# Graph attention: 32 blocks of 128 destinations, taken from two halves of the nodes, in place of 33 blocks of 125

## Chip, core and metric

The kernel runs on one NeuronCore of a Trainium2 chip. The metric is the device time of one execution in microseconds; the median of three runs stands for the kernel. The inputs come from a fixed seed, so every run has the same graph.

## What is computed

One layer of graph attention: 4096 nodes with 64 features, 50,000 edges, 4 heads of 64 output features. Cut to what matters:

```python
x_proj[h] = x @ weight[h]                                # 4 heads
score[h, e] = sum(x_proj[h, src] * att_src[h]) + sum(x_proj[h, dst] * att_dst[h])
score = where(score > 0, score, 0.2 * score)
output[h, dst] += exp(score[h, e]) * x_proj[h, src]      # over the edges e
output[h, dst] /= sum(exp(score[h, e]) over edges to dst) + 1e-8
return output as (4096, 256)
```

## The kernel before

**Two sorts.** Every edge becomes one number, `key`, that holds its source group (16 groups of 256 sources), its destination and its source within the group (lines 700 to 702, in two halves, as the edge list lands). VectorE sorts the keys: `Sorter.rows` sorts each of the 128 rows, `runs` merges 8 rows into each of 16 runs. The sorted runs go to DRAM, each source group is gathered from all 16 runs by an indirect DMA (`group`, lines 365 to 381), and a second sort puts each group's edges in order of destination. Beside the second sort ScalarE counts, for each boundary between blocks of destinations, the keys below it (`below`, line 270: one pass per boundary), TensorE sums these counts, and VectorE turns them into the places where each block begins (`Stretches`).

**Tables.** While the first sort runs, `tables` (lines 383 to 424) prepares what the blocks need: `xT`, the transposed node features, and with it the attention terms of the sources in `xa` and of the destinations in `adb` (line 420, one matmul per 128 sources and one per block of destinations).

**Windows.** A block of destinations meets each of the 16 source groups in one window of `W2` = 128 sorted edges. Eight blocks' windows are fetched by one indirect DMA (line 362), so there are `NI` = ceil(33 / 8) = 5 of them. `unpack(i)` splits the keys of eight blocks into destination and source (two VectorE and two GpSimd instructions, lines 441 to 446) and SyncE stores them to `gat_bins` (line 447).

**Blocks.** `Blocks.run` (line 583) walks over `ND` = 33 blocks of `BD` = 125 destinations; the last has 96. For a block, `load` (line 469) brings its 16 windows to all 128 partitions (1 MB, by SyncE's queue, four buffers), `onehot` (lines 493, 495) compares them with the partition's number, `gather` (lines 514 to 524) lets TensorE pick the features and attention terms of the 16 x 128 edges by one-hot matmuls, and ScalarE takes the exponential and copies `xs` out of PSUM. `weights` and `values` (lines 534, 543) multiply; `sums` (lines 561, 568) adds up the edges of a destination: 16 matmuls for the denominator and 2 x 16 whose moving operand is the one-hot `xs[:, t, 0:BD]`. `Finish` copies the sum out (line 624), projects it with the weights (line 636), divides (lines 641, 649) and stores the rows (line 651). In the last block the two halves are kept apart (`parts`), so that the end of the kernel is short.

The order of the work is written out by hand. In `run`, iteration `b` does `values(b)`, `gather(b + 1)`, `onehot(b + 2)`, `load(b + 4)`, the projection of block `b - 1`, and at last `sums(b)`; iterations 1 and 2 end with `unpack(3)` and `unpack(4)`. SyncE issues its DMAs in that order and holds what stands behind one that waits.

At the end VectorE's word `over` says whether a window was longer than 128 edges (`longest`, lines 746 and 747). If it was, the part below line 776 does the whole aggregation again in loops.

Of the kernel before, what the change touches and what calls it, by code (L numbers as in the profile page):

```python
# [26 lines left out]
W2 = 128  # L27
BD = 125
FINE = 2
# [9 lines left out]
def kernel(ctx: ExitStack, tc: tile.TileContext, x: bass.AP, edge_index: bass.AP,  # L39
# [343 lines left out]
    def tables(pr, pps, pp1):  # L383
# [25 lines left out]
        S.copy(out=xa[:, :, 2 * H:XC], in_=xf[:])  # L409
        xT = pr.tile([Din, ND * BD + P - BD], F32)  # L410
        G.memset(xT[:, N:], 0.0)
        for q in range(NB // 4):
            ps = pps.tile([Din, 4, P], F32, tag="pp")
            for i in range(4):
                T.transpose(out=ps[:, i, :], in_=xf[:, 4 * q + i, :], identity=ident[:])
            S.copy(out=xT[:, 4 * q * P:4 * (q + 1) * P], in_=ps[:])
        for k, (n, step, to) in enumerate(((NB, P, xa[:, :, 0:2 * H]), (ND, BD, adb[:, :, P:AB]))):
            ps = pp1.tile([P, n, H], F32, name=f"at_ps{k}")
            for b in range(n):
                T.matmul(out=ps[:, b, :], lhsT=xT[:, b * step:b * step + P], rhs=uv[:, k, :], start=(b == 0), stop=True,  # L420
                         skip_group_check=True)
            S.copy(out=to[:, :, 0:H], in_=ps[:])
            S.mul(out=to[:, :, H:2 * H], in_=ps[:], mul=ALPHA)
# [30 lines left out]
    class Blocks:  # L454
# [93 lines left out]
        def sums(self, b, k):  # L548
# [3 lines left out]
            if k < 0:  # L552
                self.acc = self.psa.tile([P, AW], F32, name="acc")
                self.to = [self.acc[:, i * BD:(i + 1) * BD] for i in range(2)]
                self.n = BD
                if apart:
                    self.n = N - b * BD
                    self.to = [self.psx.tile([P, CH[0][1], PW], F32, name="ps")[:, 0, 0:self.n] for i in range(2)]
                wv = self.wv.pop(b)
# [7 lines left out]
            for t in range(NT):  # L567
                T.matmul(out=self.to[k], lhsT=val[:, t, k * P:(k + 1) * P], rhs=xs[:, t, 0:self.n],  # L568
                         start=apart and t == 0, stop=(t == NT - 1), skip_group_check=True)
# [39 lines left out]
    class Finish:  # L609
# [29 lines left out]
        def invert(self, b):  # L639
            self.inv = self.fp.tile([P, H], F32, name="inv")  # L640
            V.reciprocal(out=self.inv[0:BD], in_=self.den.pop(b)[0:BD, 2 * BD:AW])

        def give(self, b, parts=1):
            res = self.fp.tile([P, H, Dout], F32, name="res")
            m = min(BD, N - b * BD)
            nh = H // parts
            for k, eng in zip(range(parts), (nc.sync, nc.scalar)):
                h = slice(k * nh, (k + 1) * nh)
                V.tensor_tensor(out=res[0:m, h], in0=av(self.pf[0:m], k * nh * Dout, [Dout, nh], [1, Dout]),
                                in1=av(self.inv[0:m], k * nh, [1, nh], [0, Dout]), op=OP.mult)  # L650
# [34 lines left out]
    with tc.tile_pool(name="sort1", bufs=1) as so1, tc.tile_pool(name="pre", bufs=1) as pr, \  # L685
            tc.tile_pool(name="pps", bufs=2, space=PSUM) as pps, \
            tc.tile_pool(name="pp1", bufs=1, space=PSUM) as pp1:
        sli = so1.tile([P, EL], I32)
        uF = so1.tile([P, EL], F32)
        key = so1.tile([P, L], F32)  # L690
        so = Sorter(so1, key)
# [3 lines left out]
        for e, n in ((0, EH), (EH, EL - EH)):  # L695
# [139 lines left out]
```

## Time and profile before

| | us |
|---|---|
| median of 3 runs | 287.45 |
| lowest and highest of them | 287.11, 287.89 |
| profiled execution, span (its time with what lies around the span isn't listed apart) | 286.5 |

| engine | busy us | share of the span | instructions |
|---|---|---|---|
| TensorE, matmuls | 202.4 | 71% | 3524 |
| TensorE, weight loads | 192.9 | 67% | 3524 |
| VectorE | 259.0 | 90% | 529 |
| ScalarE | 190.8 | 67% | 392 |
| GpSimd | 44.0 | 15% | 81 |

The busy time is an average over stages of quite different kinds. Up to about 112 us the program sorts; from about 128 us to 275 us it walks over the blocks; the rest is the end of the last block and its stores. What bounds each stage is read from the stage's own rows.

### The profile page before, as it was taken

Reading aid. Unit: us, or ns where it says so; the run is one execution under the profiler, and the core shown is the slowest. Engines: PE = TensorE matmul, PEld = TensorE weight load, DVE = VectorE, ACT = ScalarE, POOL = GpSimd, SP = SyncE. Lnnn points to the kernel's source line nnn. Section 1 sums busy time; section 2 is a strip of 40 time slices with the busy share of each in tenths; the row PEclk is TensorE's granted clock in tenths of the full one; section 3 lists DMA queues with packets and bytes.
Section 4 is the critical chain, followed back from the end, with each engine's and each line's share of the span. In section 5 each row is a group of like instructions: output and inputs, shape, how many; then the busy total and the mean of one; then the engine's idle time right before and its main releaser. Section 6 shows DMA issues by size and latency. Waiting matters only on the chain.

```text
span 286.5 us, 8520 instructions
## 1 busy us (share of the span) xinstructions
PE 202.4 (71%) x3524; PEld 192.9 (67%) x3524; DVE 259.0 (90%) x529; ACT 190.8 (67%) x392; POOL 44.0 (15%) x81
## 2 busy tenths in 40 slices
PE   0010899980000046699998999999999999999990
PEld 0010589980000024489998999999999999999980
DVE  5999999994499999899997999999999999999970
ACT  2960620014499956688787888888888888888860
POOL 7883000001100000868700000000000000000000
PEclk9999975555555559999999999999999999999996
DMA  3017000001100001296698576768676767775011
GB/s 112 0 32 136 0 2 0 0 1 38 37 0 0 0 0 40 55 382 207 215 326 321 190 291 214 298 202 302 209 288 222 282 220 282 231 264 188 21 38 43
DMA packets 12687, 40.75 MB, mean 142 GB/s; under 512 B 1840, under 2 KB 8272, under 8 KB 8672
## 3 DMA queue, kind: packets, MB, share of 16 engines
q1 hardware_dynamic: 10128, 37.91, 37.4%
q10 hardware_dynamic: 1808, 1.56, 2.4%
q0 software_dynamic: 704, 0.66, 1.1%
q8 instruction: 29, 0.48, 0.7%
q14 instruction: 18, 0.15, 0.2%
HBM read 35.08 MB, written 5.05 MB: 140 GB/s over the span
## 4 chain that ended last, share of the span: by engine, by line


## 5 line engine op out<-in xcount | busy, mean ns | idle before, releaser
L524 ACT CAST xs<-ps 128x1200 bf16<-128x1200 f32 (+1 forms) x99 | 104.1, 1052 | 0.0
L543 DVE TENSOR_TENSOR val<-xs,wv 128x4096 bf16<-128x4096 bf16 (+3 forms) x37 | 75.6, 2051 | 0.4 <-ACT xs L524 0.2
L568 PE MATMUL acc<-xs,val 128*128 128x125 bf16 x1024 | 62.0, 218 | 1.2 <-issue 1.2
L516 PE MATMUL ps<-adb,oh 128*128 128x136 bf16 x528 | 61.3, 223 | 0.0
L514 PE MATMUL ps<-xa,oh 128*128 128x72 bf16 x528 | 58.8, 196 | 1.7 <-ACT bc L481 1.1
L568 PEld LDWEIGHTS <-val 128*128 128x128 bf16 x1056 | 58.5, 98 | 1.6 <-issue 1.3
L516 PEld LDWEIGHTS <-oh 128*128 128x128 bf16 x528 | 49.0, 98 | 1.5 <-issue 1.4
L514 PEld LDWEIGHTS <-oh 128*128 128x128 bf16 x528 | 47.0, 98 | 1.0 <-DVE oh L493 0.9
L281 PE MATMUL cnt_ps<-sgn,sel 128*128 128x17 f32 (+1 forms) x6 | 1.6, 386 | 59.9 <-ACT sgn L273 40.6
L493 DVE TENSOR_SCALAR oh<-bc,pF 128x4096 bf16<-128x4096 bf16 (+2 forms) x37 | 42.4, 1146 | 0.8 <-ACT bc L481 0.8
L281 PEld LDWEIGHTS cnt_ps<-sgn,sel 128*128 128x128 f32 x6 | 1.4, 318 | 60.0 <-issue 60.0
L522 ACT ACTIVATE ex<-ps 128x96 bf16<-128x96 f32 (+1 forms) x99 | 25.0, 252 | 21.2 <-PE ps L520 21.0
L202 DVE TENSOR_TENSOR sA<-sB 128x256 f32<-128x256 f32 (+2 forms) x104 | 37.2, 399 | 1.5
L202 DVE TENSOR_TENSOR sB<-sA 128x256 f32<-128x256 f32 (+2 forms) x98 | 35.1, 399 | 1.3
L520 PE MATMUL ps<-xa,oh 128*128 128x72 bf16 x528 | 33.3, 197 | 0.1
L520 PEld LDWEIGHTS <-oh 128*128 128x128 bf16 x528 | 26.3, 99 | 0.2 <-DVE oh L495 0.2
L420 PEld LDWEIGHTS at_ps<-uv,xT 64*128 64x128 f32 x130 | 26.0, 311 | 0.2 <-issue 0.2
L420 PE MATMUL at_ps<-uv,xT 64*128 64x4 f32 x130 | 26.1, 338 | 0.0
L495 DVE TENSOR_SCALAR oh<-bc,pF 128x2048 bf16<-128x2048 bf16 (+2 forms) x37 | 25.6, 692 | 0.0
L270 ACT ACTIVATE junk<-kr,nb 128x512 f32<-128x512 f32 x33 | 23.8, 722 | 1.1
L636 PE MATMUL pf<-Wbd,aT 128*128 128x128 f32 x128 | 21.9, 294 | 0.5 <-ACT aT L624 0.5
L561 PEld LDWEIGHTS <-xs 128*128 128x128 bf16 x528 | 18.6, 96 | 1.0 <-issue 0.6
(143 smaller groups left out, 237.3 us busy)
## 6 DMA issues: line engine op xcount, KB each, us to landing
bc<-gat_bins SPq DMA_DIRECT2D x31, 1024.0 KB, 5.1
out_dram<-res SPq DMA_DIRECT2D x32, 125.0 KB
eD<-in_edge_index_dram ACTq DMA_DIRECT2D x2, 195.0 KB, 3.5
eS<-in_edge_index_dram SPq DMA_DIRECT2D x2, 195.0 KB
gat_bins<-tb SPq DMA_DIRECT2D x5, 64.0 KB, 4.8
gat_sorted<-sA SPq DMA_DIRECT2D x1, 256.0 KB, 2.0
gat_sorted<-ki SPq DMA_DIRECT2D x1, 256.0 KB
win<-gat_sorted,to POOLq DMA_INDIRECT x5, 7.9
```

Source lines behind the costliest of these rows:

```text
L202: V.tensor_tensor(out=av(d[:], o, [2 * h, n], [1, h]), in0=av(s[:], 0, [2 * h, n], [1, h]), in1=av(s[:], h, [2 * h, n], [1, h]), op=op)
L270: S.activation(out=junk[:], in_=v, func=ACTF.Sign, bias=nbnd[:, b:b + 1], scale=1.0, accum_out=sgn[:, b:b + 1])
L420: T.matmul(out=ps[:, b, :], lhsT=xT[:, b * step:b * step + P], rhs=uv[:, k, :], start=(b == 0), stop=True, skip_group_check=True)
L493: V.tensor_scalar(out=oh[:, e], in0=bc[:, e], scalar1=pF[:, 0:1], scalar2=None, op0=OP.is_equal)
L495: V.tensor_scalar(out=av(oh[:], (2 * NT + t0) * W2, [W2, nt], [1, W2]), in0=av(bc[:], (2 * t0 + 1) * W2, [2 * W2, nt], [1, W2]), scalar1=p ...
L514: T.matmul(out=ps[:, i, P:P + XC], lhsT=hot(2 * t + 1), rhs=xa[:, 2 * t, :], start=(i % 2 == 0), stop=False, skip_group_check=True)
L516: T.matmul(out=ps[:, i, 0:S0], lhsT=hot(2 * t), rhs=adb[:, b, :], start=False, stop=False, skip_group_check=True)
L520: T.matmul(out=ps[:, i, P:P + XC], lhsT=hot(2 * NT + t), rhs=xa[:, 2 * t + 1, :], start=False, stop=True, skip_group_check=True)
L522: S.activation(out=av(ex[:], 2 * t0, [2, n], [2 * NT, 2 * H], [1, 2]), in_=av(ps[:], P, [PW, n], [1, 2 * H], [0, 2]), func=ACTF.Exp)
L524: S.copy(out=xs[:, t0:t0 + n, 0:P + XC], in_=ps[:, 0:n, 0:P + XC])
L543: V.tensor_tensor(out=av(val[:], h * Dout + t * C, [Dout, nh], [C, n], [1, Din]), in0=av(xs[:], S0 + t * XW, [0, nh], [XW, n], [1, Din]), ...
L568: T.matmul(out=self.to[k], lhsT=val[:, t, k * P:(k + 1) * P], rhs=xs[:, t, 0:self.n], start=apart and t == 0, stop=(t == NT - 1), skip_gro ...
```

## The change

`BD` becomes 128, so that there are 32 blocks, `NI` becomes 4, and every block is full. A block now holds 64 nodes of the lower half and the matching 64 of the upper half, in turn: node n < 2048 has the place 2n, node n >= 2048 the place 2(n - 2048) + 1. The key is built from the place instead of the node's number (two more instructions in each half of the edge list), `xT` is written in the order of places and read back with a step of two for the sources, and the store of a block's rows goes to 64 rows of each half. The code for a short last block goes away.

```diff
-BD = 125
+BD = 128
...
-        xT = pr.tile([Din, ND * BD + P - BD], F32)
-        G.memset(xT[:, N:], 0.0)
+        xT = pr.tile([Din, N], F32)
+        place = lambda n: 2 * n % N + 2 * n // N
...
-            S.copy(out=xT[:, 4 * q * P:4 * (q + 1) * P], in_=ps[:])
+            S.copy(out=av(xT[:], place(4 * q * P), [2, 4 * P]), in_=av(ps[:], 0, [1, 4 * P]))
...
-                T.matmul(out=ps[:, b, :], lhsT=xT[:, b * step:b * step + P], rhs=uv[:, k, :], start=(b == 0), stop=True,
+                T.matmul(out=ps[:, b, :], lhsT=nodes(b), rhs=uv[:, k, :], start=(b == 0), stop=True,
...
-                T.matmul(out=self.to[k], lhsT=val[:, t, k * P:(k + 1) * P], rhs=xs[:, t, 0:self.n],
+                T.matmul(out=self.to[k], lhsT=val[:, t, k * P:(k + 1) * P], rhs=xs[:, t, 0:BD],
...
-                eng.dma_start(out=out[b * BD:b * BD + m, k * nh * Dout:(k + 1) * nh * Dout],
-                              in_=res[0:m, h].rearrange("p h o -> p (h o)"))
+                eng.dma_start(out=out.rearrange("(c b a) e -> b a c e", c=2, b=ND)[b, :, :, k * nh * Dout:(k + 1) * nh * Dout],
+                              in_=res[:, h].rearrange("p h o -> p (h o)"))
...
+            V.tensor_scalar(out=dF[:, c], in0=dst, scalar1=float(N // 2), scalar2=-float((N - 1) * SG), op0=OP.is_ge,
+                            op1=OP.mult)
             V.scalar_tensor_tensor(out=uF[:, c], in0=sli[:, c], scalar=float(N - 1), in1=src, op0=OP.mult, op1=OP.add)
-            V.scalar_tensor_tensor(out=key[:, c], in0=dst, scalar=float(SG), in1=uF[:, c], op0=OP.mult, op1=OP.add)
+            V.scalar_tensor_tensor(out=kF[:, c], in0=dst, scalar=float(2 * SG), in1=dF[:, c], op0=OP.mult, op1=OP.add)
+            V.tensor_tensor(out=key[:, c], in0=uF[:, c], in1=kF[:, c], op=OP.add)
```

VectorE's queue at the start of the program, where the keys of the two halves are built and the first sort begins:

```order
-L700 TENSOR_SCALAR sli<-eS 128x195
-L701 SCALAR_TENSOR_TENSOR uF<-sli,eS 128x195
-L702 SCALAR_TENSOR_TENSOR key<-eD,uF 128x195
+L701 TENSOR_SCALAR dF<-eD 128x195
+L703 SCALAR_TENSOR_TENSOR uF<-sli,eS 128x195
+L704 SCALAR_TENSOR_TENSOR kF<-eD,dF 128x195
+L705 TENSOR_TENSOR key<-uF,kF 128x195
```

Each half has two instructions more (`dF` and the addition at the end), and `key` now waits for two chains, one from the source and one from the destination.

SyncE's queue at the start of the blocks, before the change. A row of line 447 is the store of an `unpack`, one of line 469 the load of a block's windows (`x3`: three in a row), one of line 651 the store of a finished block:

```order
L447 DMA gat_bins<-tb 128x256
L469 DMA bc<-gat_bins 128x4096 x3
L447 DMA gat_bins<-tb 128x256 x2
L469 DMA bc<-gat_bins 128x4096
L651 DMA out_dram<-res 125x256
L447 DMA gat_bins<-tb 128x256
L469 DMA bc<-gat_bins 128x4096
L651 DMA out_dram<-res 125x256
L447 DMA gat_bins<-tb 128x256
L469 DMA bc<-gat_bins 128x4096
```

The same place with the change (lines 448, 470 and 649 are the same three kinds):

```order
L448 DMA gat_bins<-tb 128x256
L470 DMA bc<-gat_bins 128x4096 x3
L448 DMA gat_bins<-tb 128x256 x2
L470 DMA bc<-gat_bins 128x4096
L649 DMA out_dram<-res 64x2x256
L448 DMA gat_bins<-tb 128x256
L470 DMA bc<-gat_bins 128x4096
L649 DMA out_dram<-res 64x2x256
L470 DMA bc<-gat_bins 128x4096
```

The store of the fifth `unpack` is gone, so the load of block 7 stands right behind the store of block 1's rows.

## Rows read from the trace of the kernel before

**Rows 1.** Busy time of each engine in 160 to 180 us, `--windows` view, with TensorE's clock

```profile
160.00:180.00 20.00, 20.00 (x431) 19.95 (x429) 19.87 (x27) 16.66 (x35) 0.00 (x0) 1.00 0.72 255
```

**Rows 2.** Waits between engines, 160 to 270 us: total us, times, longest

```profile
ACT ex L522 <- PE ps L520: 14.7, 47, 0.4
```

**Rows 3.** Timeline, VectorE: line 543 in the first and last regular block; one block's `onehot`, `weights`

```profile
158.38 2.28 DVE L543 TENSOR_TENSOR val<-xs,wv 128x4096 bf16<-128x4096 bf16 x1
...
207.79 1.26 DVE L493 TENSOR_SCALAR oh<-bc,pF 128x4096 bf16<-128x4096 bf16 x1
209.08 0.22 DVE L534 TENSOR_TENSOR wv<-ex 128x128 bf16<-128x128 bf16 x1
...
271.49 2.28 DVE L543 TENSOR_TENSOR val<-xs,wv 128x4096 bf16<-128x4096 bf16 x1
```

**Rows 4.** Timeline, TensorE's matmuls in one block: start us, us, line, out<-in, count

```profile
207.22 0.36 PE L520 MATMUL ps<-xa,oh 128*128 128x72 bf16 x6
207.42 0.20 PE L514 MATMUL ps<-xa,oh 128*128 128x72 bf16 x1
...
207.51 0.20 PE L514 MATMUL ps<-xa,oh 128*128 128x72 bf16 x1
...
207.91 1.93 PE L568 MATMUL acc<-xs,val 128*128 128x125 bf16 x32
209.68 0.20 PE L514 MATMUL ps<-xa,oh 128*128 128x72 bf16 x1
```

**Rows 5.** Timeline, VectorE, the second half of the keys and the first sorting steps

```profile
5.52 0.27 DVE L700 TENSOR_SCALAR sli<-eS 128x196 int32<-128x196 int32 x1 [0.39 <-DMA eS<-in_edge_index_dram]
...
6.22 0.36 DVE L702 SCALAR_TENSOR_TENSOR key<-eD,uF 128x196 f32<-128x196 int32 x1
6.62 0.36 DVE L191 TENSOR_TENSOR sA<-key 128x196 f32<-128x196 f32 x1
6.90 0.36 DVE L193 TENSOR_TENSOR sA<-key 128x196 f32<-128x196 f32 x1
```

**Rows 6.** Timeline, VectorE, iteration 2's end (`unpack(4)`) and the blocks 3, 4 and 6

```profile
137.40 0.21 DVE L441 TENSOR_SCALAR t<-win 128x128 int32<-128x128 int32 x1
...
137.66 2.28 DVE L543 TENSOR_TENSOR val<-xs,wv 128x4096 bf16<-128x4096 bf16 x1
...
142.79 2.28 DVE L543 TENSOR_TENSOR val<-xs,wv 128x4096 bf16<-128x4096 bf16 x1
...
152.38 2.28 DVE L543 TENSOR_TENSOR val<-xs,wv 128x4096 bf16<-128x4096 bf16 x1
```

**Rows 7.** Timeline, TensorE, 139 to 160 us: the rows with idle time before them

```profile
139.03 0.35 PE L561 MATMUL acc<-wv,xs 128*128 128x4 bf16 x8 [0.54 <-issue]
152.27 1.04 PE L568 MATMUL acc<-xs,val 128*128 128x125 bf16 x16 [1.15 <-issue]
```

**Rows 8.** Timeline, SyncE's queue: block 1's rows, then the last `unpack` store

```profile
138.21 0.29 SPq L651 DMA_DIRECT2D out_dram<-res  x1
141.70 0.32 SPq L447 DMA_DIRECT2D gat_bins<-tb  x1
```

**Rows 9.** Timeline, ScalarE, TensorE and VectorE: the tables and the counts beside the sorts

```profile
37.49 26.14 PE L420 MATMUL at_ps<-uv,xT 64*128 64x4 f32 x130
...
75.23 0.72 ACT L370 ACTIVATE kr<-raw,goff 128x512 f32<-128x512 f32 x1 [7.52 <-DMA raw<-gat_sorted,wi]
...
106.91 0.19 DVE L318 TENSOR_SCALAR cnt<-cnt_ps 128x41 f32<-128x41 f32 x1
```

**Rows 10.** The end: timeline of ScalarE, the last part's copy

```profile
278.90 0.24 ACT L628 COPY part<-ps 128x96 f32<-128x96 f32 x1 [0.53 <-PE ps L568]
```

**Rows 11.** TensorE's warm-up and its next work (timeline), and the clock beside it (`--windows`)

```profile
104.65 3.62 PE L722 MATMUL warm<-adb,identb 128*128 128x512 bf16 x9
109.42 1.47 PE L479 MATMUL ps<-tb,identb 128*128 128x256 bf16 x12 [1.14 <-ACT tb L735]
...
108.00:110.00 2.00, 0.86 (x8) 0.52 (x6) 2.00 (x9) 0.41 (x1) 0.00 (x0) 1.00 0.00 0
```

More of the change, by code (lines that the diff above doesn't have):

```diff
@@ L415, in tables @@
                 T.transpose(out=ps[:, i, :], in_=xf[:, 4 * q + i, :], identity=ident[:])
-            S.copy(out=xT[:, 4 * q * P:4 * (q + 1) * P], in_=ps[:])
-        for k, (n, step, to) in enumerate(((NB, P, xa[:, :, 0:2 * H]), (ND, BD, adb[:, :, P:AB]))):
+            S.copy(out=av(xT[:], place(4 * q * P), [2, 4 * P]), in_=av(ps[:], 0, [1, 4 * P]))
+        for k, (n, nodes, to) in enumerate(((NB, lambda b: av(xT[:], place(b * P), [2, P]), xa[:, :, 0:2 * H]),
+                                            (ND, lambda b: xT[:, b * BD:(b + 1) * BD], adb[:, :, P:AB]))):
             ps = pp1.tile([P, n, H], F32, name=f"at_ps{k}")
             for b in range(n):
-                T.matmul(out=ps[:, b, :], lhsT=xT[:, b * step:b * step + P], rhs=uv[:, k, :], start=(b == 0), stop=True,
+                T.matmul(out=ps[:, b, :], lhsT=nodes(b), rhs=uv[:, k, :], start=(b == 0), stop=True,
                          skip_group_check=True)
@@ L554, in sums @@
                 self.to = [self.acc[:, i * BD:(i + 1) * BD] for i in range(2)]
-                self.n = BD
                 if apart:
-                    self.n = N - b * BD
-                    self.to = [self.psx.tile([P, CH[0][1], PW], F32, name="ps")[:, 0, 0:self.n] for i in range(2)]
+                    self.to = [self.psx.tile([P, CH[0][1], PW], F32, name="ps")[:, 0, 0:BD] for i in range(2)]
                 wv = self.wv.pop(b)
@@ L640, in invert @@
             self.inv = self.fp.tile([P, H], F32, name="inv")
-            V.reciprocal(out=self.inv[0:BD], in_=self.den.pop(b)[0:BD, 2 * BD:AW])
+            V.reciprocal(out=self.inv[:], in_=self.den.pop(b)[:, 2 * BD:AW])
         def give(self, b, parts=1):
             res = self.fp.tile([P, H, Dout], F32, name="res")
-            m = min(BD, N - b * BD)
             nh = H // parts
@@ L648, in give @@
                 h = slice(k * nh, (k + 1) * nh)
-                V.tensor_tensor(out=res[0:m, h], in0=av(self.pf[0:m], k * nh * Dout, [Dout, nh], [1, Dout]),
-                                in1=av(self.inv[0:m], k * nh, [1, nh], [0, Dout]), op=OP.mult)
-                eng.dma_start(out=out[b * BD:b * BD + m, k * nh * Dout:(k + 1) * nh * Dout],
-                              in_=res[0:m, h].rearrange("p h o -> p (h o)"))
+                V.tensor_tensor(out=res[:, h], in0=av(self.pf[:], k * nh * Dout, [Dout, nh], [1, Dout]),
+                                in1=av(self.inv[:], k * nh, [1, nh], [0, Dout]), op=OP.mult)
+                eng.dma_start(out=out.rearrange("(c b a) e -> b a c e", c=2, b=ND)[b, :, :, k * nh * Dout:(k + 1) * nh * Dout],
+                              in_=res[:, h].rearrange("p h o -> p (h o)"))
     class Total:
@@ L689 @@
         uF = so1.tile([P, EL], F32)
+        dF = so1.tile([P, EL], F32)
+        kF = so1.tile([P, EL], F32)
         key = so1.tile([P, L], F32)
```

## Prediction, written before the change was timed

> **What bounds the kernel now.** I read the busy time by stretch first, then the waits, then the timelines of the engines that come out nearest to full. In the middle of the walk over the blocks, matmuls cover the whole of 20 us and VectorE is busy in 19.87 of them; ScalarE has 3.3 us to spare [rows 1]. Two engines look full, so the waits must tell them apart: in 110 us there is one kind of wait at all, ScalarE's `ex` on TensorE's `ps` [rows 2]. VectorE has a small one that the list is too coarse for: the record of `onehot` ends at 207.79 + 1.26 = 209.05, and `weights`, which needs the last `ex`, starts at 209.08, with no overlap [rows 3]. The reader is to see in this that VectorE follows ScalarE, and ScalarE follows TensorE.
>
> TensorE's own pace says the same. From block 7 to block 31 the `values` instruction comes every (271.49 - 158.38) / 24 = 4.713 us [rows 3]. In a block the six 72-column matmuls of line 520 take (207.42 - 207.22) / 6 = 33 ns each, a pair of 72 and 136 columns takes 207.51 - 207.42 = 90 ns, and the 32 matmuls of 125 columns take (209.68 - 207.91) / 32 = 55.3 ns each, each right behind the last [rows 4]. The time of one grows with its columns: (55.3 - 33) / (125 - 72) = 0.42 ns per column. **The blocks are bound by TensorE**, and VectorE is close behind it. Before the blocks, VectorE's two sorts set the time, and there every added instruction on VectorE counts in full.
>
> **The change, part by part.**
>
> *One block less.* 33 blocks become 32, and a regular one goes: -4.71 us.
>
> *Wider blocks.* Lines 514, 516, 520, 561 and 636 keep their columns; the 32 matmuls of line 568 go from 125 to 128. That is 32 x 3 x 0.42 ns = 0.04 us for a block, and the period becomes 4.753 us. From block 3 on TensorE sets it, so 28 intervals pay it: +1.1 us. VectorE's and ScalarE's instructions run over 128 partitions with the same number of elements in each (`aT` has 256 columns for 250), and stay behind TensorE. The bounds are 0 (if VectorE's pace were the true bound) and 2.2 us (twice the slope).
>
> A rule speaks against this step. The Trainium skill ("TensorE: Matmul & The Clock Gate", section "Back-to-back issue gap") gives about 81 ns for each matmul in a sustained stream of weight loads and 128-column matmuls. By it the 32 would take 0.8 us more in each block; it is a rival below.
>
> *The keys.* VectorE gets two more instructions in each half. In the first half they lie in the 0.39 us for which VectorE waits for the second half of the edge list [rows 5], as long as the destinations land with the sources. In the second half nothing covers them. Instructions that wait for the one before come every (6.62 - 6.22) = 0.40 us, two that don't depend on each other every (6.90 - 6.62) = 0.28 us [rows 5]. `sli`, `dF` and `uF` hardly wait for each other, so I take +0.4; the bounds are 0.3 and 0.8. It passes in full to everything behind it, because VectorE sorts without a gap.
>
> *The fifth window.* One indirect DMA, one store and `unpack(4)` go. The two VectorE instructions of it take 137.66 - 137.40 = 0.26 us at the end of iteration 2 [rows 6]. Without them VectorE would need 4.63 us, and TensorE's 4.75 decides, against 4.89 now: -0.14. GpSimd's part was nobody's wait except SyncE's.
>
> *SyncE's queue.* The store of `unpack(4)` waits until 141.70 for GpSimd, and the load of block 7 stands behind it in the queue; the store of rows ahead of it went out at 138.21 [rows 8]. Now the load goes at about 138.6, some 3 us earlier and right behind that of block 6. No engine waited for that load, so by itself this is 0. But twice TensorE stops in the middle of a run of equal matmuls, for 0.54 and 1.15 us, "issue" being all the profile names [rows 7]. The intervals around them are 5.13 us (137.66 to 142.79) and 6.00 us (152.38 to 158.38 [rows 3, 6]) in place of 4.71, so they cost 0.4 and 1.3 us. Nothing in the program waits there; the transfers of this stretch are the nearest thing that could, since no such stop comes after it, where loads go out one per block. The second stop lies behind the loads of blocks 7 and 8, which went out close together; these are now drawn apart. I take half of its 1.3 us, -0.6, with 0 and -1.7 (both stops gone) as the bounds, and +1.3 if a new one comes where the loads of blocks 6 and 7 meet.
>
> *The end.* The last block has 128 destinations in place of 96. Its 32 matmuls grow by 32 x 0.42 = 13 ns each, 0.43 us, most of it on the path since the copy of the last part waits for them [rows 10]. The copy, the projection's weights and two stores a third larger add something like 0.1: +0.5 us, between 0.2 and 0.8.
>
> *At nothing.* ScalarE's 33 passes become 32, and the small copy behind them goes: VectorE reads the counts at 106.91, after TensorE has finished with them and its warm-up is under way [rows 9, 11], so nobody waits for it. Two of 130 matmuls of the tables go, and half of the rest read their weights with a step of two. They have 26.14 us for 130, 0.2 us each, and ScalarE waits 7.52 us afterwards for the gathered keys [rows 9]; if each of the 64 took twice as long, ScalarE's passes would be 5.3 us late, of which the counts' slack and the missing pass take some 3; the rest, 2 us, is inside the range. The rows' stores go to two regions; SyncE has time for them.
>
> *Sum:* -4.71 + 1.1 + 0.4 - 0.14 - 0.6 + 0.5 = -3.45 us. The profiled span of 286.5 becomes 283.05. The median of the runs is 287.45, 0.95 us above that span for what lies around it; I keep this: **284.0 us**. What a measurement of this kernel can tell from no change is about 0.3%, 0.86 us, so faster means below 286.6.
>
> **The rivals.**
>
> *The stops grow or move* (chance 0.12). The load of block 7 now meets that of block 6, and TensorE stops there. For: both stops lie in the stretch in which the loads are dense. Against: from 160 us on a load per block does no harm. With +1.3 in place of -0.6 the time is 285.9.
>
> *The stops go* (0.18). All of 1.7 us in place of 0.6: 282.9. For: the load that crowded the stretch is drawn forward, and less is stored. The Trainium skill ("DMA: Bandwidth & Descriptors", section "Why a DMA increments its semaphore by 16 and not by 1") speaks for it: a transfer is spread over the largest number of engines up to 16 that divides its outer dimensions, which is 5 for 125 rows and 16 for 128. By that rule a block's store no longer crowds five of the engines; no row here shows single engines.
>
> *Slower: TensorE's clock falls before the blocks start* (0.03). The warm-up of line 722 brings it up: in 108 to 110 us it is 1.00, and it stays there over a pause of 1.14 us [rows 11]. Now one pass of ScalarE is left out, of the shape that takes 0.72 us in [rows 9], so against VectorE the counts and the warm-up come at least 0.7 us earlier. The first work behind the warm-up waits for VectorE, and the pause grows to about 2 us. If the clock falls to 1.2 GHz in it, the work of about two blocks up to 128 us runs at half speed. That is up to 2 x 4.71 us, half of which other engines may hide: 284.0 + 4.7 to 9.4, 289 to 293. It decides from a loss of 2.6 us on. Against it: the counter-example of 1.14 us, and that the work behind the pause is dense.
>
> *Slower: wider matmuls fall into another rate* (0.01). By the rule of 81 ns, 31 blocks x 32 x (81 - 56.5) ns = 24 us more: 308. Against it: the 136-column matmuls, whose pair with a 72-column one takes 90 ns together and 90 - 33 = 57 ns alone, weight loads included [rows 4]. The trace has the rate on both sides of 128 columns, and the rule doesn't hold here.
>
> *The second pass runs* (0.01). A window longer than 128 edges makes the program do everything again, at least 32 more blocks of 4.7 us, beyond 430 us. Counted from the inputs, the fullest window of the 512 holds 125 edges, and 128 once its ends are rounded to fours; the test is for more than 128. It holds, with nothing to spare.
>
> **How the numbers follow.** The forecast has 0.65, with 283.2 to 285.0 as its own range (keys, end and column cost at their bounds). With the two cases of the stops 95 in 100 are covered; the range of 282.6 to 285.9 reaches to both and leaves out their far ends. Faster takes the forecast, the stops gone, and most of the stops moved: 0.92. A stop that costs more than two microseconds beyond the forecast ends within 0.3%: 0.03. The three cases of the other side have 0.05.
>
> **What would show it.** The interval of line 543 in the middle should be 4.75 us and there should be 24 or 25 equal ones; 4.71 would say that columns cost nothing or that VectorE sets the pace, above 4.8 that the rate is wrong. The first sorting step should start 0.4 us later than 6.62, and the gathered keys arrive as much later. Idle time before line 568 or 561 with "issue" shows what became of the stops. The clock should be 1.00 from before 112 us to the end of the blocks. The part copies should come some 0.4 us later behind the last `values`. The prediction is wrong if the time is above 286.6 or below 282.6: then either the stretch before the blocks or their period isn't what the rows say.

## The result, and the profile after

The changed kernel takes 282.5 us (median of 4 runs, 282.19 to 282.72), the kernel before 287.28 us in the runs beside it (4 runs, 286.51 to 287.89). The ratio is 0.984, with an interval of 0.981 to 0.987: 4.8 us faster, where 3.45 us were forecast (284.0 us).

The head of the page and TensorE's clock by slices, of the changed kernel:

```profile
span 280.6 us, 8284 instructions
...
PE 200.1 (71%) x3422; PEld 190.7 (68%) x3422; DVE 254.9 (91%) x525; ACT 186.2 (66%) x381; POOL 36.5 (13%) x75
...
PEclk9999975555555557699999999999999999999998
```

The new thing in it is the "76" around 105 to 119 us: the clock falls again after the warm-up had brought it up, where it had stayed up before (0.50 in these rows is the lower of the clock's two levels, 1.2 GHz, and 1.00 the upper one, 2.4 GHz). Busy time by stretch (`--windows`: start and end, length, busy time and count of TensorE's matmuls, its weight loads, VectorE, ScalarE, GpSimd, then the clock):

```profile
108.00:110.00 2.00, 0.21 (x2) 0.19 (x2) 2.00 (x9) 0.41 (x1) 0.00 (x0) 1.00 0.00 0
110.00:112.00 2.00, 1.83 (x12) 1.22 (x10) 2.00 (x9) 1.36 (x2) 0.00 (x0) 0.63 0.01 4
112.00:114.00 2.00, 1.54 (x11) 1.03 (x11) 1.84 (x7) 2.00 (x3) 0.00 (x0) 0.50 0.30 118
...
120.00:122.00 2.00, 1.08 (x11) 0.83 (x9) 2.00 (x2) 1.66 (x2) 0.00 (x0) 1.00 0.48 107
...
160.00:180.00 20.00, 20.00 (x426) 19.95 (x423) 19.82 (x28) 16.93 (x36) 0.00 (x0) 1.00 0.71 259
```

The last line is [rows 1] over again, to within 0.05 us for VectorE. The waits from 160 to 262 us are of one kind too, as in [rows 2]:

```profile
ACT ex L523 <- PE ps L521: 12.7, 43, 0.4
```

VectorE's timeline of the changed kernel: the keys and the first sorting step, `values` of the blocks 1 to 4, one block in the middle, and the end:

```profile
3.90 0.29 DVE L700 TENSOR_SCALAR sli<-eS 128x195 int32<-128x195 int32 x1 [1.69 <-DMA eS<-in_edge_index_dram]
...
6.82 0.36 DVE L191 TENSOR_TENSOR sA<-key 128x196 f32<-128x196 f32 x1
...
128.19 2.30 DVE L544 TENSOR_TENSOR val<-xs,wv 128x4096 bf16<-128x4096 bf16 x1
...
133.12 2.28 DVE L544 TENSOR_TENSOR val<-xs,wv 128x4096 bf16<-128x4096 bf16 x1
...
137.75 2.28 DVE L544 TENSOR_TENSOR val<-xs,wv 128x4096 bf16<-128x4096 bf16 x1
...
142.49 2.28 DVE L544 TENSOR_TENSOR val<-xs,wv 128x4096 bf16<-128x4096 bf16 x1
...
203.48 0.42 DVE L647 TENSOR_TENSOR res<-pf,inv 128x256 f32<-128x256 f32 x1
203.82 2.28 DVE L544 TENSOR_TENSOR val<-xs,wv 128x4096 bf16<-128x4096 bf16 x1
...
265.14 2.28 DVE L544 TENSOR_TENSOR val<-xs,wv 128x4096 bf16<-128x4096 bf16 x1
269.44 2.56 DVE L544 TENSOR_TENSOR val<-xs,wv 128x2048 bf16<-128x2048 bf16 x5 [0.15 <-ACT xs L525]
...
273.77 0.49 DVE L647 TENSOR_TENSOR res<-pf,inv 128x128 f32<-128x128 f32 x2 [1.07 <-PE pf L635]
```

From block 4 to the last regular block the interval is (265.14 - 142.49) / 26 = 4.717 us, where 4.753 was forecast and [rows 3] gave 4.713. TensorE's timeline of the changed kernel, the work behind the warm-up and then one block:

```profile
109.79 2.04 PE L480 MATMUL ps<-tb,identb 128*128 128x256 bf16 x12 [2.19 <-ACT tb L738]
...
203.85 0.36 PE L521 MATMUL ps<-xa,oh 128*128 128x72 bf16 x6
204.04 0.68 PE L635 MATMUL pf<-Wbd,aT 128*128 128x128 f32 x4
...
206.22 1.95 PE L567 MATMUL acc<-xs,val 128*128 128x128 bf16 x32
208.01 0.20 PE L515 MATMUL ps<-xa,oh 128*128 128x72 bf16 x1
```

The 32 wide matmuls take (208.01 - 206.22) / 32 = 55.9 ns each, against 55.3 in [rows 4]. They did grow. The interval didn't follow.

**Where the 5.9 us between the two profiled spans lie** (286.5 and 280.6). `values` of block 1 starts at 128.19 in place of 127.84: +0.35. From there to the last block there is one interval less (-4.71), 28 of them are 0.0044 us longer (+0.12), the work of `unpack(4)` is gone (-0.18: the interval with it took 4.89 in place of 4.63 us, and the one behind it gave back 0.08, being 4.62 or 4.63 us where no stop lies in it, as in two of the runs below), and none of the stops of [rows 7] is there. By the same intervals those had cost 0.50 and 1.29 us, and a smaller one between them 0.17, 1.96 in all. From the last block's first `values` to the end the changed kernel takes 280.6 - 269.44 = 11.16 us; before it was 10.71 (the same instruction started at 275.79): +0.45. The sum is -5.9.

### The profile page after: what moved, and what is told of

The parts are those of the page before. It is cut to its first block, busy times and chain, and to the rows that moved or that the text cites. A ratio compares the mean times of both kernels' runs of the same rounds, so it can differ in the third digit from the quotient of the medians.

```text
span 280.6 us, 8284 instructions
## 1 busy us (share of the span) xinstructions
PE 200.1 (71%) x3422; PEld 190.7 (68%) x3422; DVE 254.9 (91%) x525; ACT 186.2 (66%) x381; POOL 36.5 (13%) x75
## 4 chain that ended last, share of the span: by engine, by line
## 5 line engine op out<-in xcount | busy, mean ns | idle before, releaser
L525 ACT CAST xs<-ps 128x1200 bf16<-128x1200 f32 (+1 forms) x96 | 100.9, 1051 | 0.0
L544 DVE TENSOR_TENSOR val<-xs,wv 128x4096 bf16<-128x4096 bf16 (+3 forms) x36 | 73.3, 2044 | 0.4 <-ACT xs L525 0.2
L567 PE MATMUL acc<-xs,val 128*128 128x128 bf16 x992 | 60.7, 219 | 0.0
L515 PE MATMUL ps<-xa,oh 128*128 128x72 bf16 x512 | 58.1, 198 | 0.8 <-ACT bc L482 0.7
L567 PEld LDWEIGHTS <-val 128*128 128x128 bf16 x1024 | 57.8, 98 | 0.2
L517 PEld LDWEIGHTS <-oh 128*128 128x128 bf16 x512 | 48.3, 99 | 0.9 <-issue 0.8
L515 PEld LDWEIGHTS <-oh 128*128 128x128 bf16 x512 | 46.2, 99 | 0.7 <-DVE oh L494 0.7
L494 DVE TENSOR_SCALAR oh<-bc,pF 128x4096 bf16<-128x4096 bf16 (+2 forms) x36 | 41.2, 1145 | 0.2 <-ACT bc L482 0.2
L523 ACT ACTIVATE ex<-ps 128x96 bf16<-128x96 f32 (+1 forms) x96 | 24.1, 252 | 19.9 <-PE ps L521 19.8
L521 PE MATMUL ps<-xa,oh 128*128 128x72 bf16 x512 | 32.9, 199 | 0.1
L521 PEld LDWEIGHTS <-oh 128*128 128x128 bf16 x512 | 26.0, 100 | 0.2 <-DVE oh L496 0.2
L496 DVE TENSOR_SCALAR oh<-bc,pF 128x2048 bf16<-128x2048 bf16 (+2 forms) x36 | 24.9, 691 | 0.0
L270 ACT ACTIVATE junk<-kr,nb 128x512 f32<-128x512 f32 x32 | 23.1, 722 | 1.0
```

The source lines that it names most:

```text
L270: S.activation(out=junk[:], in_=v, func=ACTF.Sign, bias=nbnd[:, b:b + 1], scale=1.0, accum_out=sgn[:, b:b + 1])
L494: V.tensor_scalar(out=oh[:, e], in0=bc[:, e], scalar1=pF[:, 0:1], scalar2=None, op0=OP.is_equal)
L496: V.tensor_scalar(out=av(oh[:], (2 * NT + t0) * W2, [W2, nt], [1, W2]), in0=av(bc[:], (2 * t0 + 1) * W2, [2 * W2, nt], [1, W2]), scalar1=p ...
L515: T.matmul(out=ps[:, i, P:P + XC], lhsT=hot(2 * t + 1), rhs=xa[:, 2 * t, :], start=(i % 2 == 0), stop=False, skip_group_check=True)
L517: T.matmul(out=ps[:, i, 0:S0], lhsT=hot(2 * t), rhs=adb[:, b, :], start=False, stop=False, skip_group_check=True)
L521: T.matmul(out=ps[:, i, P:P + XC], lhsT=hot(2 * NT + t), rhs=xa[:, 2 * t + 1, :], start=False, stop=True, skip_group_check=True)
```

## The experiments

Two questions were open: what the stops of [rows 7] are and whether the change removes them, and why wider matmuls cost nothing. Each kernel is compared with the kernel before on its own chip, whose median differs from chip to chip (288.96, 289.37 and 286.62 us).

### The stops: the queue's hold, or the stores

*The hold taken out of the kernel before.* `unpack(4)` moves to the end of iteration 12:

```diff
-        blocks.run(1, {i - 2: lambda i=i: win.unpack(i) for i in range(3, NI)})
+        blocks.run(1, {1: lambda: win.unpack(3), 12: lambda: win.unpack(4)})
```

> The kernel before, with the last window's unpacking moved from the end of iteration 2 to that of iteration 12, so that its store no longer holds the load of block 7. Theory 1 (the two stops of TensorE come from the loads that this hold pushes together): the stops at line 561 and 568 are gone, the intervals of 5.1 and 6.0 us become about 4.7, the span falls by 1.3 to 1.9 us and the time as much. Theory 2 (they come from the stores of 125 rows, which crowd some DMA engines): the stops stay, no change in time beyond 0.3 us. Theory 3 (the stops belong to the one profiled execution, not to the timed ones): the span falls and the time does not.

288.93 us, ratio 1.001 (0.998 to 1.004). No stop as in [rows 7] is in the profile, and no time was gained. The moved `unpack` shows as one interval of 4.99 us and one of 4.63. In this profiled execution the clock took what the missing stops had given (below).

*The hold put back into the changed kernel.* A second `unpack(3)` at the end of iteration 2:

```diff
-        blocks.run(1, {i - 2: lambda i=i: win.unpack(i) for i in range(3, NI)})
+        blocks.run(1, {1: lambda: win.unpack(3), 2: lambda: win.unpack(3)})
```

> The changed kernel, with the hold put back: the end of iteration 2 unpacks the fourth window once more and stores it again (the same bytes), so that the load of block 7 again stands behind a store that waits for GpSimd. Theory 1: the two stops come back, the span grows by 0.15 us for VectorE's two instructions and by 1.3 to 1.9 us for the stops. Theory 2: only the 0.1 to 0.3 us of VectorE come back. Theory 3: the span may change and the time changes by 0.1 to 0.3 us only.

284.95 us, ratio 0.986 (0.981 to 0.990). No stop as in [rows 7] is in the profile. One interval of 4.91 us is all there is, and there VectorE waits 0.21 us for the load of block 6, which stands ahead of the store that was put back. In this execution the hold made no stop.

*The stores of the kernel before in two pieces*, of 112 and 13 rows:

```diff
-                eng.dma_start(out=out[b * BD:b * BD + m, k * nh * Dout:(k + 1) * nh * Dout],
-                              in_=res[0:m, h].rearrange("p h o -> p (h o)"))
+                for r in ((0, 112), (112, 125)) if m == BD else ((0, m),):
+                    eng.dma_start(out=out[b * BD + r[0]:b * BD + r[1], k * nh * Dout:(k + 1) * nh * Dout],
+                                  in_=res[r[0]:r[1], h].rearrange("p h o -> p (h o)"))
```

> The kernel before, with each store of 125 rows cut in two, of 112 and 13 rows. Theory 2: the stops go or shrink, span 1.3 to 1.9 us shorter. Theory 1: the stops stay, nothing changes beyond 0.3 us; SyncE issues 31 DMAs more, which it has time for.

287.81 us, ratio 0.995 (0.993 to 0.998): a small gain, and no stop in the profile. The rest of the walk is as long there as in the kernel before (last table below), so where the gain lies isn't shown. The direction fits the Trainium skill ("DMA: Bandwidth & Descriptors", section "Why a DMA increments its semaphore by 16 and not by 1"), by which 112 rows go over 16 of the engines and 125 over 5. No view here shows single engines, so for that cause the ratio is all there is.

*The changed kernel once more, unchanged,* on another chip:

> The changed kernel once more, as the measure for the runs beside it on the same chip. Expected: ratio to the kernel before 0.984, as measured. Its profile has another phase of the clock: if TensorE's clock before the blocks differs from execution to execution, the start of block 1 (128.2 us in the first profile) moves by up to 2.5 us, while the interval of the blocks stays 4.717 us.

284.74 us, ratio 0.984 (0.980 to 0.988): the same ratio as at first. But this profiled execution has a stop. TensorE's timeline, and behind it VectorE's:

```profile
139.51 0.41 PE L560 MATMUL acc<-wv,xs 128*128 128x4 bf16 x10
...
140.54 0.31 PE L560 MATMUL acc<-wv,xs 128*128 128x4 bf16 x6 [0.62 <-issue]
```

```profile
138.74 2.27 DVE L544 TENSOR_TENSOR val<-xs,wv 128x4096 bf16<-128x4096 bf16 x1
...
144.25 2.28 DVE L544 TENSOR_TENSOR val<-xs,wv 128x4096 bf16<-128x4096 bf16 x1
```

It lies inside the same run of sixteen equal matmuls as the first stop of [rows 7], in the interval of the same block, in a program that has neither the hold nor stores of 125 rows. So neither is needed for it. These stops come and go between executions of either kernel.

*What TensorE waits for in them.* "issue" says that the profile shows nothing, but the kept traces have the place of each stop and the transfers of a queue of the kind "instruction", 16 KB each (of the kernel before; packets, MB, share):

```profile
q8 instruction: 29, 0.48, 0.7%
```

Count TensorE's recorded instructions (matmuls, weight loads and those of its sequencer) by their starts. The stops of [rows 7] then come behind 1217 and 1729 of them, the one above behind 1218, one of 0.93 us in the kernel with the new keys behind 962, and one of 0.24 us in the run that moves `res` (both below) behind 1729: always a multiple of 256 apart, to within one. In these five, and in two of under 0.2 us that come behind 1473, TensorE goes on 1.3 to 1.5 us after a transfer of that queue has ended. At all the other places of this series up to 3009, in the 13 traces of this document without a second pass, 1.6 us or more have gone by since the last transfer, and TensorE doesn't stop. So the stops are waits for instructions that come late. That such a transfer holds 256 instructions of TensorE is inferred from the spacing; why some come late isn't shown.

*A second kind of stop* has its cause named, a load that lands late. VectorE's `onehot` waits for it in the kernel before with its own columns and twice in the changed kernel with both additions to the warm-up (both below):

```profile
153.01 1.28 DVE L493 TENSOR_SCALAR oh<-bc,pF 128x4096 bf16<-128x4096 bf16 x1 [0.70 <-DMA bc<-gat_bins]
```

```profile
141.71 1.29 DVE L494 TENSOR_SCALAR oh<-bc,pF 128x4096 bf16<-128x4096 bf16 x1 [0.80 <-DMA bc<-gat_bins]
...
146.94 1.29 DVE L494 TENSOR_SCALAR oh<-bc,pF 128x4096 bf16<-128x4096 bf16 x1 [0.52 <-DMA bc<-gat_bins]
```

The first is the load of block 7, which went out at 145.51 behind the store of `unpack(4)` and took 7.4 us. Issued right behind the rows' store at 141.15, it would have landed in time even so (an estimate from these numbers). So the hold did cost something there, in one of six profiled executions that have it. The other two are the loads of the blocks 5 and 6 in a kernel without `unpack(4)`. They took 8.4 and 8.0 us, where the median of that profile is 5.8.

### The columns: why the interval stays at 4.717 us

In the kernel before there is a small gap that the prediction overlooked. TensorE's timeline of the kernel before, one block earlier than [rows 4]:

```profile
203.20 1.93 PE L568 MATMUL acc<-xs,val 128*128 128x125 bf16 x32
204.96 0.20 PE L514 MATMUL ps<-xa,oh 128*128 128x72 bf16 x1
...
205.51 0.36 PE L520 MATMUL ps<-xa,oh 128*128 128x72 bf16 x6
205.74 0.68 PE L636 MATMUL pf<-Wbd,aT 128*128 128x128 f32 x4
```

Six matmuls of 33 ns take 0.20 us, but the projection of line 636 starts 0.23 us behind the first of them. With the change this step is 204.04 - 203.85 = 0.19. About 0.03 us a block that TensorE had stood still, without the waits naming it, went to the wider matmuls: in this block they take (204.96 - 203.20) / 32 = 55.0 ns, and 32 x (55.9 - 55.0) ns is 0.03 us too. What did TensorE stand still for?

*Its weights' columns.* In the kernel before, the projection of each half reads 128 columns, of which three belong to what lies behind its own 125 (the second half, and the denominators, which another instruction writes later); here it reads its own 125:

```diff
-                self.aT[b] = [t[:, k * BD:k * BD + P] for k in range(2)]
+                self.aT[b] = [t[:, k * BD:(k + 1) * BD] for k in range(2)]
```

> The kernel before, with the projection reading only the 125 columns of its own half of aT. Before, the second half's 128 columns reached 3 columns into the denominators, so the projection had to wait for the instruction that writes them. Theory: TensorE's step from line 520 to line 636 falls from 64 ns to 40 ns as in the changed kernel, the interval of a block from 4.713 to about 4.69 us, and the span by 28 x 0.024 = 0.7 us. Rival (the 25 ns have another cause, such as the place of aT in memory): no change in the step, and none in time.

288.08 us, ratio 0.998 (0.994 to 1.001); the step is still 0.22 us (207.12 to 207.34), the interval 4.707. This was not the cause.

*`res`.* VectorE reads the last projection out of `pf` before the next may write it. Moved ahead of the second `onehot`, it is done earlier:

```diff
-                self.onehot(b + 2, halves=(1,))
...
+                self.onehot(b + 2, halves=(1,))
```

(the first line stood before `give(b - 1)`, which divides and stores; now it stands behind it.)

> The kernel before, with the division and store of a finished block moved ahead of the second half of the one-hot comparison on VectorE. Theory 1 (a block's interval is set by a loop through three engines: the projection waits for VectorE to have read the last projection, then the gather of the second chunk, ScalarE's copy and exponential, VectorE's weights, second comparison and division; TensorE has 32 ns to spare in it): the step from line 520 to line 636 falls from 64 to about 32 ns, the interval from 4.713 to 4.68 us, the span by 28 x 0.03 = 0.9 us. Theory 2 (TensorE is full at 4.713 us, as the prediction had it): the interval stays 4.713.

290.94 us, ratio 1.007 (1.002 to 1.012): slower. TensorE's and VectorE's timeline:

```profile
206.94 0.37 PE L520 MATMUL ps<-xa,oh 128*128 128x72 bf16 x6
207.14 0.69 PE L636 MATMUL pf<-Wbd,aT 128*128 128x128 f32 x4
...
211.77 0.37 PE L520 MATMUL ps<-xa,oh 128*128 128x72 bf16 x6
```

```profile
210.64 0.42 DVE L649 TENSOR_TENSOR res<-pf,inv 125x256 f32<-125x256 f32 x1
210.97 0.74 DVE L495 TENSOR_SCALAR oh<-bc,pF 128x2048 bf16<-128x2048 bf16 x1
211.63 2.29 DVE L543 TENSOR_TENSOR val<-xs,wv 128x4096 bf16<-128x4096 bf16 x1
```

The step fell to 0.20 us: the projection no longer waits, so `res` had held it. The latency says the same. VectorE's timeline of the kernel before, for the projection at 205.74 above:

```profile
205.18 0.42 DVE L649 TENSOR_TENSOR res<-pf,inv 125x256 f32<-125x256 f32 x1
```

The projection starts 0.14 us behind the end of `res` (205.60), and in the changed kernel too (203.90 and 204.04). In every block from 160 to 262 us of both it is 0.145 to 0.148 us. With `res` moved it is 0.92. But now the six matmuls of line 520 wait for the second `onehot`, which ends at 210.97 + 0.74 = 211.71, and the interval is 211.63 - 206.80 = 4.83 us (the `values` before started at 206.80). VectorE's order sets the pace of TensorE here as in the kernel before; an instruction moved forward there moves the wait to what was moved back.

*More columns.* The wide matmuls of the changed kernel with 136 columns, eight of them never read:

```diff
+    BX = BD + 8
...
-                self.acc = self.psa.tile([P, AW], F32, name="acc")
-                self.to = [self.acc[:, i * BD:(i + 1) * BD] for i in range(2)]
+                self.acc = self.psa.tile([P, 2 * BX + H], F32, name="acc")
+                self.to = [self.acc[:, i * BX:(i + 1) * BX] for i in range(2)]
...
-                T.matmul(out=self.to[k], lhsT=val[:, t, k * P:(k + 1) * P], rhs=xs[:, t, 0:BD],
+                T.matmul(out=self.to[k], lhsT=val[:, t, k * P:(k + 1) * P], rhs=xs[:, t, 0:BX],
```

> The changed kernel, with 136 columns in each of the 32 matmuls of a block's sums instead of 128 (the 8 extra columns are summed up and never read). Theory 1 (TensorE had 32 ns to spare before, the wider blocks took 29 of them): now the rest is gone, so the extra columns count in full, 32 x 8 x 0.3 to 0.42 ns = 0.08 to 0.11 us for a block; the interval becomes 4.79 to 4.82 us and the span grows by 1.9 to 2.8 us. Rival (the three extra columns cost nothing because TensorE has much more to spare): the interval stays below 4.73.

286.97 us, ratio 0.994 (0.989 to 0.998), and 2.2 us more than the changed kernel beside it. TensorE's and VectorE's timeline:

```profile
206.68 0.69 PE L636 MATMUL pf<-Wbd,aT 128*128 128x128 f32 x4
...
208.86 2.06 PE L568 MATMUL acc<-xs,val 128*128 128x136 bf16 x32
210.76 0.20 PE L516 MATMUL ps<-xa,oh 128*128 128x72 bf16 x1
```

```profile
206.01 0.42 DVE L648 TENSOR_TENSOR res<-pf,inv 128x256 f32<-128x256 f32 x1
206.35 2.28 DVE L545 TENSOR_TENSOR val<-xs,wv 128x4096 bf16<-128x4096 bf16 x1
...
211.17 2.28 DVE L545 TENSOR_TENSOR val<-xs,wv 128x4096 bf16<-128x4096 bf16 x1
```

59.4 ns for each matmul, 3.5 more than with 128 columns, and an interval of 4.82 us: 0.10 more, nearly all of 32 x 3.5 ns = 0.11. The projection now starts 0.25 us behind the end of `res` (206.43 and 206.68) and no longer waits for it. From 128 columns on TensorE is full to within 0.01 us, and columns count; the first three were paid out of the gap.

### The clock before the blocks

*A longer warm-up in the changed kernel*, 14 matmuls in place of 9, and four more beside the second part of block 1's windows, in front of its `onehot`:

```diff
-            busy(9)
+            busy(14)
...
             if c == 1:
+                busy(4)
                 blocks.onehot(1, *CH[0])
```

> The changed kernel, with 14 warm-up matmuls instead of 9 behind the counts, and 4 more in the pause between the second and the third spread of block 1. Theory (the clock falls in some executions in the two pauses before the blocks, which costs up to 2.5 us): the clock stays at full from the warm-up on, the span to block 1 falls to 127.5 us or less, and the time is 0.3 to 1.5 us below that of the changed kernel, with less spread from run to run. Rival (the clock's fall costs nothing because other engines hide it): same time as the changed kernel within 0.3 us.

282.98 us, ratio 0.980 (0.975 to 0.984), though its profiled execution has the two late loads shown above, worth 0.76 and 0.51 us. The clock is 1.00 from 108 us on. On another chip the same kernel again, and the first of the two lines alone:

> The version with both additions once more, beside the one with the longer warm-up alone. Theory (both pauses matter): ratio 0.979 to 0.980, below that of the longer warm-up alone by 0.1 to 0.4%. Rival (the four matmuls hold up the third spread of block 1): above it.

> The changed kernel with 14 warm-up matmuls instead of 9 behind the counts and no others. Theory (the pause behind the warm-up, which grew from 1.1 to 2 us, is where the change lets the clock fall): the first spread of block 0 runs at full clock, block 0's values start some 0.5 to 1 us earlier than in the changed kernel, time 0.3 to 1.5 us below it, ratio 0.979 to 0.983. Rival (the four later matmuls did it): ratio 0.984.

281.84 us, ratio 0.983 (0.981 to 0.986), and 282.32 us, ratio 0.986 (0.984 to 0.988). The first ran in 281.55 to 281.86 us, the narrowest spread of all kernels, and is the fastest version here, on the chip where the kernel before is fastest too. Both miss the ratios that their theories gave. The longer warm-up alone lies above the changed kernel's 0.984, not at 0.979 to 0.983, so no gain from it is shown. The two additions together lie 0.3% below it, but the changed kernel wasn't run on this chip, and the intervals of all these overlap with that of the changed kernel (0.980 to 0.988): a gain is possible but not shown. Its stretch of 110 to 112 us, beside the second row above:

```profile
110.00:112.00 2.00, 1.22 (x12) 0.94 (x10) 2.00 (x9) 1.40 (x2) 0.00 (x0) 1.00 0.01 4
```

The twelve matmuls take 1.22 us at a clock of 1.00 and 1.83 us at 0.63.

### The keys alone, and the order of the nodes

*The new keys and tables in the kernel before,* still 33 blocks of 125 (the rows come out in the order of places):

```diff
+        place = lambda n: 2 * n % N + 2 * n // N
...
-            S.copy(out=xT[:, 4 * q * P:4 * (q + 1) * P], in_=ps[:])
+            S.copy(out=av(xT[:], place(4 * q * P), [2, 4 * P]), in_=av(ps[:], 0, [1, 4 * P]))
...
-            V.scalar_tensor_tensor(out=key[:, c], in0=dst, scalar=float(SG), in1=uF[:, c], op0=OP.mult, op1=OP.add)
+            V.scalar_tensor_tensor(out=kF[:, c], in0=dst, scalar=float(2 * SG), in1=dF[:, c], op0=OP.mult, op1=OP.add)
+            V.tensor_tensor(out=key[:, c], in0=uF[:, c], in1=kF[:, c], op=OP.add)
```

> The kernel before, 33 blocks of 125, with the changed kernel's keys and tables alone: the destinations go by their places, the features are written in that order and read back with a step of two. The rows of the output stay in the order of the places instead of that of the nodes. Theory: from the first instruction of the keys to the first sorting step 2.9 us instead of 2.5, which moves everything behind it, 0.4 us more (ratio about 1.0014); the strided reads of the tables cost nothing. Rival (the strided weight loads are twice as slow and their lateness reaches the counts): 2 us more, ratio about 1.007.

287.28 us, ratio 1.002 (1.000 to 1.004): +0.6 us. From the first key instruction to the first sorting step 2.91 us pass, 2.92 in the changed kernel above, against 2.55 before. The tables take 25.57 us in place of 26.14 [rows 9], so reading weights with a step of two costs nothing.

*The changed kernel with its nodes in plain order:*

```diff
-        place = lambda n: 2 * n % N + 2 * n // N
+        place = lambda n: n
...
-            V.tensor_scalar(out=dF[:, c], in0=dst, scalar1=float(N // 2), scalar2=-float((N - 1) * SG), op0=OP.is_ge,
+            V.tensor_scalar(out=dF[:, c], in0=dst, scalar1=float(N // 2), scalar2=0.0, op0=OP.is_ge,
...
-            V.scalar_tensor_tensor(out=kF[:, c], in0=dst, scalar=float(2 * SG), in1=dF[:, c], op0=OP.mult, op1=OP.add)
+            V.scalar_tensor_tensor(out=kF[:, c], in0=dst, scalar=float(SG), in1=dF[:, c], op0=OP.mult, op1=OP.add)
```

> The changed kernel with blocks of 128 destinations in the order of the nodes, without the two halves (the two added instructions on the keys stay, with a factor that makes them neutral). Counted from the inputs, the fullest window then spans 132 edges, over the 128 of a window. Theory: the second pass runs, with 32 blocks more for each of two offsets, in loops that nothing overlaps; the time is above 580 us. Rival (the test does not fire): 282 to 285 us.

785.09 us. The head of its page:

```profile
span 782.9 us, 22676 instructions
```

The fullest window spans 132 edges by the count from the inputs, the second pass runs, and the instructions go from 8284 to 22676. On this graph blocks of 128 in plain order don't fit windows of 128 edges, and those from two halves do.

### What differs between executions

Two things vary from one execution to the next: when the second block's `values` starts, and the stops behind it. The clock (`--windows`) from 122 to 128 us goes with most of the first. The stops, of both kinds, are the intervals beyond the regular ones:

| kernel | clock, 122 to 128 us | `values` of block 1 at | stops, us | span, us | span less both |
|---|---|---|---|---|---|
| before | 1.00 | 127.84 | 1.96 | 286.5 | 156.7 |
| before, `unpack(4)` late | 0.72 | 130.71 | 0 | 287.6 | 156.9 |
| before, stores split | 0.72 | 129.37 | 0 | 286.3 | 156.9 |
| before, own columns | 0.72 | 130.64 | 0.69 | 287.9 | 156.6 |
| before, new keys | 1.00 | 128.65 | 0.92 | 285.9 | 156.3 |
| changed | 1.00 | 128.19 | 0 | 280.6 | 152.4 |
| changed, again | 1.00 | 129.18 | 0.91 | 282.5 | 152.4 |
| changed, second `unpack(3)` | 0.72 | 130.58 | 0.19 | 283.7 | 152.9 |
| changed, 14 | 1.00 | 127.69 | 0 | 280.0 | 152.3 |
| changed, 14 and 4 | 1.00 | 128.99 | 1.27 | 282.7 | 152.4 |
| changed, 14 and 4, again | 1.00 | 127.47 | 0 | 279.8 | 152.3 |

(The kernels with another interval or a second pass are left out.) In the kernel with `unpack(4)` late, the row of the second column is

```profile
122.00:128.00 6.00, 4.34 (x64) 4.13 (x64) 4.81 (x13) 4.08 (x4) 0.63 (x2) 0.72 0.92 343
```

Where the clock falls there, block 1's `values` start at 129.4 to 130.7 us (mean 130.3); where it doesn't, at 127.5 to 129.2 (mean 128.3). Of the kernels left out, the one that moves `res` has 0.72 too and 129.15 us, so the start alone doesn't tell. The step from the `values` of block 0 to those of block 1 does: 10.4 to 10.7 us in the five executions with the fall, 8.7 to 9.8 in the eight without. The last column is the rest of the walk and the end, freed of both: 156.3 to 156.9 us with 33 blocks, 152.3 to 152.4 with 32 (152.9 with a second `unpack(3)` in it). The difference of about 4.3 us is the sum of the terms behind that point: -4.71 + 0.12 - 0.18 + 0.45.

## Why the prediction was right in sign and too small

**One block less** was right: -4.71 us, and 4.717 for what is left.

**The number** came out at the edge of what was forecast. The range was 282.6 to 285.9 us, and the prediction called itself wrong below 282.6. Measured were 282.50, with the kernel before at 287.28 beside it; the ratio of 0.984 on the forecast's 287.45 gives 282.85. The forecast's own case, 283.2 to 285.0, was missed. Nearest comes the rival by which the stops go (282.9), but its reason did not hold (SyncE's queue, below). That the range reached this far is luck.

**Wider blocks** is the step that failed. "The blocks are bound by TensorE ... 28 intervals pay it: +1.1 us" measured +0.12. The size of a matmul was near (55.9 ns, where the prediction has 56.5); that TensorE was full was not. [rows 4] shows one run of six matmuls without the instruction behind it, and the list of waits is too coarse for a gap of 0.03 us. The projection of line 636, which the prediction never set beside them, waited for `res`, as the run that moved `res` showed. The pace at 125 columns was that of a loop through VectorE, TensorE and ScalarE, with TensorE 0.03 us short of full. That the loop runs `res`, projection, denominators, gather, `ex`, `weights`, second `onehot` and `res` again is read from the order, and only its first link was tried. The prediction's own bound of 0 ("if VectorE's pace were the true bound") held the value.

**The rule of 81 ns** of the Trainium skill ("TensorE: Matmul & The Clock Gate", section "Back-to-back issue gap") does not hold here: 55.9 ns with 128 columns, weight loads included, in a stream that fills the engine. The same section's figure for an isolated matmul, columns / 2.4 + 2.5 ns, gives 55.8 and, at 136, 59.2; the trace has 55.9 and 59.4.

**The keys**: +0.4 forecast; 2.92 - 2.55 = +0.37 measured. **The fifth window**: -0.14 forecast, -0.18 measured. **The end**: +0.5 forecast, +0.45 measured; the step from the last `values` to `res` went from 4.00 to 4.33 us. All three terms held.

**SyncE's queue.** The load of block 7 went out at 139.15, right behind the store at 138.56, as foreseen:

```profile
138.56 0.54 SPq L649 DMA_DIRECT2D out_dram<-res  x1
139.15 2.52 SPq L470 DMA_DIRECT2D bc<-gat_bins  x1
```

But the term of -0.6 us for the stops rested on one profiled execution: they come and go between executions of either kernel, with the hold and without it. TensorE waited there for instructions and not for the loads, and taking the hold out of the kernel before gave no time. What share of the stops is in the median isn't known.

**"0.95 us above that span for what lies around it"** was wrong in the same way. In every run whose span is listed the time is 1.7 to 2.2 us above it. By that the profiled execution of the kernel before took some 288.4 us, about 1 above the median of 287.45 (its time isn't listed, so this is an estimate).

**The clock's fall** was a rival with a chance of 0.03, and its mechanism came true: a pause of 2.19 us in place of 1.14, and a clock of 0.63 and 0.50 behind it. Its price of 4.7 to 9.4 us did not. The first `values` came at 119.54 us in place of 118.49, but the second only 0.35 us later, which the keys explain by themselves. In 120 to 122 us TensorE is busy for 1.08 of 2.00 us while VectorE is busy throughout; the lost time was taken back where TensorE wasn't the bound. In the second execution of the changed kernel there was nothing to fall: the warm-up hadn't brought the clock up before the pause, and it stood at 0.50 up to 112 us.

**Summed again** with measured sizes: -4.71 + 0.12 + 0.37 - 0.18 + 0.45 = -3.95 us, against a measured -4.8 at first and -4.6 on the second chip. The intervals of the two ratios are 3.8 to 5.4 and 3.4 to 5.8 us, so the sum lies inside both, and the 0.65 to 0.85 us that are left are not clear of the noise. If they are real, their cause is open. Two things could hold them. Splitting the stores of the kernel before gave 0.5%, and by the same rule of the Trainium skill the changed kernel's stores of 128 rows are spread as widely. And the late fall of the clock, with which the second block starts some 2 us later, was seen in three of the five profiled executions of the table with 33 blocks and in one of the six with 32. But these are single executions on several chips, and the new keys alone, with no fall, gave no time back. All four of the table that show the fall ran on one chip, beside the median of 288.96 us, the one with 32 blocks among them, so the chip may decide it rather than the number of blocks.

## What to carry to other kernels

When several engines are over 99% busy, look for the place in one period where an instruction starts later than the ones ahead of it can explain; a gap of 0.03 us that no list of waits names is what decides whether added work in another engine is free. Before a stall of a profiled execution enters a forecast, see whether it can belong to that execution alone: its time against the median can say so. Look also at who released the engine behind a stall: a load that landed late and an "issue" at a fixed place in the instruction stream have nothing in common. And where a pause before a dense stretch grows, price the clock's fall by who waits in that stretch, not by the engine's own loss.

## What was unexpected of the hardware

TensorE can stop for 0.2 to 1.2 us in the middle of a run of equal matmuls, with nothing named but "issue", in some executions of a program and not in others (three of the eleven in the table have one of 0.5 us or more). These stops lie a multiple of 256 instructions apart, and TensorE goes on 1.3 to 1.5 us after a transfer of instructions has ended. Three others of the eleven have intervals that are 0.2 to 0.8 us longer because a load landed late. The clock's course before the blocks differs as much: it came up to 1.00 at 108 us in some executions and not before 118 us in another (new keys alone), and it fell again at 110 us behind a pause of 2.19 us, or at about 123 us. Together these moved the spans of the changed kernel, with either warm-up, over 2.9 us (279.8 to 282.7), more than half of what the change is worth. And three columns more in 32 matmuls of every block cost 0.004 us in an interval of 4.7, where eight more cost 0.10.
